# Issuing the probability-times-V products of up to three key blocks in one piece, in a two-layer transformer block whose instruction order a planner writes

## The chip, the cores and the metric

The kernel runs on one core of one Trainium2 chip. The metric is the device time of one execution in microseconds (us). Engines are named as the profile names them: PE is the matrix engine (TensorE), DVE is VectorE, ACT is ScalarE, POOL is GpSimd, SP is the engine whose queue issues every DMA here.

## What is computed

Two layers of a transformer block over 512 latent tokens (x) and 256 context tokens (ctx), 1024 wide, in float32. The context stream is left out after the attention keys of the second layer. Cut to what matters here:

```python
for layer in range(2):
    hx, hc = modulate(rmsnorm(x)), modulate(rmsnorm(ctx))
    # one projection, columns split into heads of 64 for three groups
    A: 6 query heads, 2 key heads; RMSNorm of q and k, rotary;  softmax(q k) v   over 768 keys
    B: 4 heads of two halves of 32; (softmax(q1 k1) - lam * softmax(q2 k2)) v, RMSNorm   over 768 keys
    C: 6 query heads, 2 key heads; 256 context keys and a band of three blocks of 128, plus a sink logit
    x += gate * (concat(A, B, C) @ w_out)                    # ctx likewise in layer 0
    x += gate * ((silu(h @ w1) * (h @ w3)) @ w2)             # ctx likewise in layer 0
return rmsnorm(x)
```

The modulation vectors come from `silu(c) @ w_ada`, 6144 columns a layer.

## The kernel before

The kernel doesn't call the engines as it goes. Every operation is recorded by a `Plan` as an `_Op` with its engine (or a choice of two: `act_dve` is ACT or DVE, `dve_pool` is DVE or POOL), its tiles and what it depends on. `schedule()` then walks through time with a price for each operation and picks, for the engine that is free first, the earliest operation that can start; operations of `together()` stay side by side. `issue()` emits the result, so all instructions have the line of its `getattr` in the profile (L347 before, L375 after the change), and rows are told apart by the names of the tiles. The order of the program is therefore decided by the prices, by the pools' sizes (`SLOTS`) and by a few offsets (`QK_AHEAD` lets score products run ahead of their place in the text).

Tiles: `u` is the pool of large SBUF buffers (4 KB a partition: weights, activations, probabilities P); `pt` holds transposed probabilities and, at the end of a layer's two halves, the gates (`gate`, read by DMA from `gscr`); `S` (2 buffers) and `T` (4 buffers of 512 columns) are in PSUM. Weights are loaded as `ws` and split into two parts `wh` and `wl` (a cast and a subtraction), and each product is made of three float32r products.

Attention goes by units: for A and B two query blocks of one pair of heads, for C one query block of all heads. Score products fill an S tile, DVE takes the maximum, ACT the exponent into P. Then P must be transposed: for each block of 128 keys PE transposes (matmuls against `ident`, 128 columns of output) into a T tile, ACT or DVE copies it to a `pt` tile, and PE multiplies V with it. One such product has 64 output partitions, so two of them (two heads) use the two halves of the array side by side; in the listing they are the rows `64x256` (A, B) and `64x384` (C), `128*64` in the profile. A product in float32 takes two passes, so a pair makes four rows in the profile. Here `acc` is the T tile that sums over key blocks:

```python
t = PT()
with plan.together():
    ...  # four transposes
pt = new("pt", [2, 256], "pt")
act_dve.copy(pt, t.rearrange("p (h n) -> p h n", h=2))
with plan.together():
    for h in range(2):
        pe.matmul(acc[64 * h:64 * h + 64, 0:256], lhsT=v_block(heads[h], kb), rhs=pt[:, h, :], ...)
```

The modulation uses products with 32 output partitions (`32x256`, four side by side). All other products have 128. In what follows a stretch of PE rows with the same number of output partitions, 64 say, between rows with another number is called a 64-row piece.

SP's queue is in order: a DMA that waits for a buffer holds up all DMAs behind it. After the last attention step of a layer come `gate_read` (the gates), the eight loads of `w_out` (`ws`), and the output projection (`T__1286`, `T__1287` are its first two result tiles in layer 0).

Of the kernel before, what the change touches and what calls it, by code (L numbers as in the profile page):

```python
# [16 lines left out]
PSUM = bass.MemoryType.PSUM  # L17
# [13 lines left out]
         "P1 P0 B P2 ABBBCAACAABCCCAAB"]  # L31
FF_TAIL = 3
FF_ADA = "dddd"
QK_AHEAD = 238
ADA_AHEAD = 300
SM_AHEAD = 39
# [4 lines left out]
COLS = {("a", "q"): (0, 384), ("a", "k"): (384, 128),  # L41
        ("b", "q0"): (640, 128), ("b", "q1"): (768, 128), ("b", "k"): (896, 256),
        ("c", "q"): (1408, 384), ("c", "k"): (1792, 128)}
SA = 0.125
SB = 32.0 ** -0.5
SLOTS = {"u": 41, "pt": 4, "s": 7, "y": 24, "rb": 2, "S": 2, "T": 4, "ropeG": 1}


class _Op:
    __slots__ = ("pos", "alts", "deps", "tiles", "dma", "gate", "tag", "boost",  # L50
                 "users", "left", "banks", "ready", "end", "eng", "calls", "at", "cost", "name")


class _Queue:
# [12 lines left out]
class Plan:  # L67
# [67 lines left out]
    def price(self, eng, method, args, kw):  # L135
        out = args[0]
        if method == "dma_start":
            return int(np.prod(out.shape)) * 4 / 360e3
        if method == "transpose":
            return 0.109  # L140
        if eng == "pe":
            n = kw["rhs"].shape[-1]
            if kw["rhs"].dtype == F32R:
                return n / 2400 + 0.003 if n >= 256 else 0.213
            share = {32: 4, 64: 2}.get(out.shape[0], 1)
            return max(n * 4 / 2400, 0.107) / share + 0.003
# [12 lines left out]
        return n * (2.5 if method == "tensor_tensor" else 1.0 if method == "memset" else 4.0) / 1200 + 0.1  # L159

    def any(self, alts):

        if self.group is not None:
            self.group.append(alts[0])
        else:
            self.add([(a[0], a, None) for a in alts])

    def add(self, alts):
        op = _Op()
        op.pos, op.tag = len(self.ops), self.label  # L170
        if alts[0][1] is None:
            calls = [o for _, _, o in alts]
            op.alts = [(calls[0][0], sum(self.price(*o) for o in calls), calls)]
        else:
            calls = [alts[0][1]]
            op.alts = [(e, self.price(*c), [c]) for e, c, _ in alts]
        op.dma = calls[0][1] == "dma_start"
# [47 lines left out]
    def schedule(self):  # L225
# [17 lines left out]
        free_at = dict.fromkeys(self.real, 0.0)  # L243
        cand = {e: [] for e in self.real}
        dma_free, now, frontier = 0.0, 0.0, 0
        done, order = [False] * n, []
# [14 lines left out]
        while len(order) < n:  # L261
            best = None
            for e in sorted(free_at, key=free_at.get):
# [4 lines left out]
                while heap and len(seen) < 250:  # L268
                    item = heapq.heappop(heap)
                    op = ops[item[1]]  # L270
                    if done[item[1]]:
                        continue
                    seen.append(item)
                    if op.gate > frontier:
                        continue
                    at, need = max(t0, op.ready, after_others(op, e)), {}
                    if any(e2 != e and max(free_at[e2], op.ready, now, after_others(op, e2)) + c2 < at + item[3]
                           for e2, c2, _ in op.alts):
                        continue
# [35 lines left out]
            if op.dma:  # L315
                free_at[e] = now + 0.5
                dma_free = max(now + 1.4, dma_free) + c
                op.end = dma_free + self.AFTER[e]
            else:
                free_at[e] = now + c  # L320
                op.end = now + c + self.AFTER[e]
            for b in op.banks:
                bank_end.setdefault(b, {})[e] = op.end
            order.append(op)
# [26 lines left out]
def dit_block(  # L351
# [26 lines left out]
    def new(tag, shape, name, dt=F32):  # L378
        return plan.tile(pools[tag], [128] + list(shape), dt, tag, nm(name))
# [10 lines left out]
    def PT():  # L390
        return new("T", [512], "T")
# [253 lines left out]
    for l in range(2):  # L645
# [33 lines left out]
        def v_block(h, kb):  # L679
            return V[kb // 2][:, kb % 2, 64 * h:64 * h + 64]  # L680
# [304 lines left out]

        def pv_pair(acc, Ps, off, heads, kbs):

            for n, kb in enumerate(kbs):
                t = PT()
                with plan.together():  # L990
                    for h in range(2):
                        for i in range(2):
                            pe.transpose(t[:, 256 * h + 128 * i:256 * h + 128 * i + 128],
                                         Ps[h][i][:, off + 128 * n:off + 128 * n + 128], ident)
                pt = new("pt", [2, 256], "pt")
                act_dve.copy(pt, t.rearrange("p (h n) -> p h n", h=2))
                with plan.together():
                    for h in range(2):
                        pe.matmul(acc[64 * h:64 * h + 64, 0:256], lhsT=v_block(heads[h], kb), rhs=pt[:, h, :],
                                  start=(n == 0), stop=(n == len(kbs) - 1))  # L1000

        def units(pairs):
            for p in pairs:
# [101 lines left out]
        def attn_c():  # L1105
# [4 lines left out]
            for r, i in ctx_first:  # L1110
# [46 lines left out]
                for n, kb in enumerate(kbs):  # L1157
                    pts = []
                    for g in range(2):
                        t = PT()  # L1160
                        with plan.together():
                            for j in range(3):
                                pe.transpose(t[:, 128 * j:128 * j + 128], Ps[g][j][:, 128 * n:128 * n + 128], ident)
                        pt = new("pt", [384], "pt")
                        act_dve.copy(pt, t[:, 0:384])
                        pts.append(pt)
                    with plan.together():
                        for g in range(2):
                            pe.matmul(acc[64 * g:64 * g + 64, 0:384], lhsT=v_block(6 + g, kb), rhs=pts[g],
                                      start=(n == 0), stop=(n == len(kbs) - 1))  # L1170
# [269 lines left out]
```

## Time and profile before

| | |
|---|---|
| median of 3 runs | 1753.08 us (1750.07 to 1755.17) |
| the profiled execution's own time | 1754.11 us |
| its span, first to last instruction | 1752.3 us |
| PE busy | 1697.7 us (97%) |
| DVE / ACT / POOL busy | 1208.2 (69%) / 615.2 (35%) / 218.1 (12%) us |
| mean granted clock of PE | 0.994 |

The rows below are from that one profiled execution. A row's busy time is from its start to its modelled end; matmuls overlap in the pipeline, so what one costs PE is read from start to start. "[0.62 <-ACT pt__1193]" behind a row is idle time of its engine before it and what ended it. Layer 0's attention lies at about 175 to 416 us, its feed-forward part at 416 to 1000, layer 1's attention at 1175 to 1345, its feed-forward part at 1390 to 1752.

### The profile page before, as it was taken

The page shows a single profiled execution, that of the slowest core. Times are in us where ns is not written, and L with a number is a line of the kernel's source. Part 1 is how long each engine was busy: PE and PEld are TensorE (multiplying, and loading weights), DVE is VectorE, ACT ScalarE, POOL GpSimd, SP SyncE. Part 2 cuts the span into 40 slices and gives each one's busy share as a digit, 9 for nine tenths or more (in the row PEclk, how much of TensorE's full clock was granted, in tenths as well). Part 3 has the DMA queues.
Part 4 walks back from the last instruction along what each step waited for, and adds up shares of the span by engine and source line. Part 5 has one row for each costly group of instructions (what it writes and reads, how often), then busy time and mean ns, then how long its engine had stood idle before and what let it go on. Part 6 is the DMA issues. An engine that isn't in the chain of part 4 may idle for free.

```text
span 1752.3 us, 24291 instructions
## 1 busy us (share of the span) xinstructions
PE 1697.7 (97%) x9426; PEld 1361.3 (78%) x9426; DVE 1208.2 (69%) x1950; ACT 615.2 (35%) x1280; POOL 218.1 (12%) x251
## 2 busy tenths in 40 slices
PE   6999898998999999999999999999999999999998
PEld 3787666676898888888888878877777888888886
DVE  3775878675567887576655765778876666676676
ACT  2523867663342122111101133157674411111111
POOL 0252200011000000000000521542001000000022
PEclk9999999999999999999999999999999999999999
DMA  9502220306363544254232342012005632332341
GB/s 314 188 27 84 67 85 20 96 11 171 96 200 101 169 159 148 93 191 136 69 108 89 105 145 72 13 31 68 1 1 157 180 109 75 106 109 81 112 144 48
DMA packets 153278, 182.96 MB, mean 104 GB/s; under 512 B 9316, under 2 KB 121396, under 8 KB 153164
## 3 DMA queue, kind: packets, MB, share of 16 engines
q1 hardware_dynamic: 153164, 181.42, 33.5%
q8 instruction: 74, 1.21, 0.3%
q14 instruction: 40, 0.33, 0.1%
HBM read 163.00 MB, written 9.47 MB: 98 GB/s over the span
## 4 chain that ended last, share of the span: by engine, by line
PE 86%; DVE 7%; issue 2%; POOL 2%; ACT 2%; DMA 2%; SPq 0%; DVEq 0%; POOLq 0%; ACTq 0%
DMA ws__1259<-in_w_out_dram 1%; PE S__1380 L347 0%; PE S__1379 L347 0%; PE S__1756 L347 0%; PE S__1561 L347 0%; PE S__1628 L347 0%; PE S__1881 L347 0%; PE S__1691 L347 0%; PE S__1823 L347 0%; PE S__1495 L347 0%; PE S__1995 L347 0%; PE S__1393 L347 0%; PE S__1967 L347 0%; PE S__1861 L347 0%; PE S__1853 L347 0%
## 5 line engine op out<-in xcount | busy, mean ns | idle before, releaser
L347 POOL TENSOR_TENSOR y__1397<-y__1397,gate__1998 128x512 f32<-128x512 f32 x1 | 1.3, 1297 | 481.0 <-DVE y__1397 L347 481.0
L347 POOL TENSOR_TENSOR ws__3491<-ws__3491,gate__3490 128x512 f32<-128x512 f32 x1 | 1.3, 1284 | 284.8 <-DMA ws__3491<-in_w_ff_dram 284.8
L347 DVE TENSOR_REDUCE t__2138<-sq__2137 128x6 f32<-128x384 f32 x1 | 0.6, 553 | 19.5 <-ACT sq__2137 L347 19.5
L347 ACT ACT_TABLE_LOAD x6 | 7.7, 1283 | 2.6 <-PE S__3040 L347 1.9
L347 ACT ACTIVATE sg__1860<-S__1853 128x768 f32<-128x768 f32 x1 | 0.8, 812 | 21.2 <-PE S__1853 L347 21.2
L347 ACT ACTIVATE sg__1914<-S__1907 128x768 f32<-128x768 f32 x1 | 0.8, 812 | 21.2 <-PE S__1907 L347 21.2
L347 ACT ACTIVATE sg__1940<-S__1933 128x768 f32<-128x768 f32 x1 | 0.8, 812 | 21.2 <-PE S__1933 L347 21.2
L347 ACT ACTIVATE sg__1966<-S__1959 128x768 f32<-128x768 f32 x1 | 0.8, 812 | 21.2 <-PE S__1959 L347 21.2
L347 DVE TENSOR_TENSOR sg__1994<-sg__1994,S__1995 128x768 f32<-128x768 f32 x1 | 1.0, 955 | 10.3 <-PE S__1995 L347 10.3
L347 ACT ACTIVATE sg__1793<-S__1786 128x768 f32<-128x768 f32 x1 | 0.8, 812 | 17.3 <-PE S__1786 L347 17.3
L347 ACT ACTIVATE sg__1665<-S__1658 128x768 f32<-128x768 f32 x1 | 0.8, 812 | 16.6 <-PE S__1658 L347 16.6
L347 PE MATMUL T__115<-wa__116,cstat 128*32 128x128 f32 x8 | 0.7, 418 | 5.7 <-DMA wa__116<-in_w_ada_dram 5.7
L347 ACT ACTIVATE xn__2033<-xf__2011 128x1024 f32<-128x1024 f32 x1 | 1.1, 1066 | 14.2 <-DVE xf__2011 L347 14.2
L347 POOL TENSOR_TENSOR ropeG<-ropeA,gqk 128x64 f32<-128x64 f32 (+1 forms) x12 | 6.0, 531 | 0.1
L347 ACT ACTIVATE sg__3107<-S__3102 128x512 f32<-128x512 f32 x1 | 0.6, 598 | 14.8 <-PE S__3102 L347 14.8
L347 ACT ACTIVATE sg__3459<-S__3454 128x512 f32<-128x512 f32 x1 | 0.6, 599 | 13.9 <-PE S__3454 L347 13.9
L347 ACT ACTIVATE sg__3173<-S__3168 128x512 f32<-128x512 f32 x1 | 0.6, 598 | 13.8 <-PE S__3168 L347 13.8
L347 ACT ACTIVATE sg__3195<-S__3190 128x512 f32<-128x512 f32 x1 | 0.6, 598 | 13.8 <-PE S__3190 L347 13.8
L347 ACT ACTIVATE sg__3217<-S__3212 128x512 f32<-128x512 f32 x1 | 0.6, 598 | 13.8 <-PE S__3212 L347 13.8
L347 ACT ACTIVATE sg__3239<-S__3234 128x512 f32<-128x512 f32 x1 | 0.6, 598 | 13.8 <-PE S__3234 L347 13.8
L347 ACT ACTIVATE sg__3261<-S__3256 128x512 f32<-128x512 f32 x1 | 0.6, 598 | 13.8 <-PE S__3256 L347 13.8
L347 ACT ACTIVATE sg__3283<-S__3278 128x512 f32<-128x512 f32 x1 | 0.6, 598 | 13.8 <-PE S__3278 L347 13.8
(14035 smaller groups left out, 6711.6 us busy)
## 6 DMA issues: line engine op xcount, KB each, us to landing
x__83<-in_x_dram SPq DMA_DIRECT2D x1, 512.0 KB
x__84<-in_x_dram SPq DMA_DIRECT2D x1, 512.0 KB
x__131<-in_x_dram SPq DMA_DIRECT2D x1, 512.0 KB, 5.9
x__136<-in_x_dram SPq DMA_DIRECT2D x1, 512.0 KB, 6.5
x__198<-in_ctx_dram SPq DMA_DIRECT2D x1, 512.0 KB
x__203<-in_ctx_dram SPq DMA_DIRECT2D x1, 512.0 KB
ws__241<-in_w_in_dram SPq DMA_DIRECT2D x1, 512.0 KB
ws__244<-in_w_in_dram SPq DMA_DIRECT2D x1, 512.0 KB
```

Source lines behind the costliest of these rows:

```text
L347: getattr(self.real[op.eng], method)(*args, **kw)
```

## The change

Three things change.

1. `pv_pair` and the loop in `attn_c` make transposes and copies for a run of key blocks first, and then record all V products of that run in one `together()`. `pv_runs` cuts the key blocks into equal runs of at most 3 (A, B) or 2 (C) blocks.
2. `pt` has 8 buffers in place of 4, `u` has 39 in place of 41.
3. The planner prices more: a change of the number of output partitions on PE costs `SWITCH` = 0.095 us in attention, and a PE candidate that stands more than `MODE_AHEAD` = 30 places further on isn't taken when the one found so far can start within `SWITCH`; an operation of DVE that reads two SBUF tensors (or copies within SBUF) and any operation of POOL are taken not to run at one time (`shares_port`); a float32r product of 512 columns is priced at 0.227 us in place of 0.216.

```diff
+PV_RUN = {"A": 3, "B": 3, "C": 2}
+SWITCH = 0.095
+MODE_AHEAD = 30
-SLOTS = {"u": 41, "pt": 4, "s": 7, "y": 24, "rb": 2, "S": 2, "T": 4, "ropeG": 1}
+SLOTS = {"u": 39, "pt": 8, "s": 7, "y": 24, "rb": 2, "S": 2, "T": 4, "ropeG": 1}
...
-                return n / 2400 + 0.003 if n >= 256 else 0.213
+                return (n + 32) / 2400 if n >= 256 else 0.213
...
+    def shares_port(self, eng, method, args, kw):
+        if eng == "pool":
+            return method != "dma_start"
+        if eng != "dve" or method == "memset":
+            return False
+        ins = [a for a in args[1:] if self.is_ap(a) and a.space != PSUM and int(np.prod(a.shape[1:])) > 1]
+        if method.startswith("tensor_scalar") or method == "tensor_copy":
+            return bool(ins) and args[0].space != PSUM
+        return len(ins) > 1
...
+                    if e == "pe" and soon is not None and item[0] > soon[1][0] + MODE_AHEAD and soon[0] <= t0 + SWITCH + 1e-9:
+                        break
...
+                    if e == "pe" and op.mode != mode and op.tag.startswith("att"):
+                        at += SWITCH
+                    if op.port[e]:
+                        at = max(at, port)
...
-            for n, kb in enumerate(kbs):
-                t = PT()
...
+            for n0, run in pv_runs(kbs, PV_RUN["A"]):
+                pts = []
+                for n in run:
+                    t = PT()
...
+                    pts.append(pt)
                 with plan.together():
+                    for n, pt in zip(run, pts):
+                        for h in range(2):
+                            pe.matmul(acc[64 * h:64 * h + 64, 0:256], lhsT=v_block(heads[h], kbs[n]), rhs=pt[:, h, :],
+                                      start=(n == 0), stop=(n == len(kbs) - 1))
+
+        def pv_runs(kbs, size):
+            m = -(-len(kbs) // size)
+            cuts = [len(kbs) * k // m for k in range(m + 1)]
+            return [(a, range(a, b)) for a, b in zip(cuts, cuts[1:])]
...
+                for n0, run in pv_runs(kbs, PV_RUN["C"]):
```

PE's order within a unit of group A in layer 0 (result tile `T__555`; `T__564` is a transpose of P, `S__618` and `S__667` are score tiles of units further on). Before:

```order
L347 MATMUL T__555<-pt__561,V__215 64x256 x2
L347 MATMUL T__564<-ident,P__543 128x128
L347 MATMUL T__564<-ident,P__549 128x128
L347 MATMUL T__564<-ident,P__544 128x128
L347 MATMUL T__564<-ident,P__550 128x128
L347 MATMUL S__618<-kx__456,qx__453 128x512
L347 MATMUL S__618<-kc__460,qx__453 128x256
L347 MATMUL S__618<-kx__457,qx__453 128x512
L347 MATMUL S__618<-kc__460,qx__453 128x256
L347 MATMUL T__555<-pt__563,V__215 64x256 x2
L347 MATMUL T__555<-pt__565,V__216 64x256 x2
```

Of the change, the same unit:

```order
L375 MATMUL T__555<-pt__557,V__214 64x256 x2
L375 MATMUL T__555<-pt__559,V__214 64x256 x2
L375 MATMUL T__555<-pt__561,V__215 64x256 x2
L375 MATMUL S__618<-kx__456,qx__453 128x512
L375 MATMUL S__618<-kc__460,qx__453 128x256
L375 MATMUL S__618<-kx__457,qx__453 128x512
L375 MATMUL S__618<-kc__460,qx__453 128x256
L375 MATMUL S__667<-kc__460,qc__458 128x256 x4
L375 MATMUL T__555<-pt__563,V__215 64x256 x2
L375 MATMUL T__555<-pt__565,V__216 64x256 x2
L375 MATMUL T__555<-pt__567,V__216 64x256 x2
```

The six pairs of `T__555` stood in five pieces and stand in two, of three pairs each; the transposes of a run now all stand ahead of its piece. Over the whole program PE has 121 64-row pieces before and 57 after, and 46 and 39 32-row pieces; the number of products is the same.

SP's order at the end of layer 0's attention (`gate` are reads of the gates, `ws` loads of `w_out`, `xr` loads of rows of the residual). Before:

```order
L347 DMA gate__1244<-gscr 128x512
L347 DMA ws__1247<-in_w_out_dram 64x1024 x2
L347 DMA ws__1250<-in_w_out_dram 64x1024 x2
L347 DMA xr__1283<-in_ctx_dram 128x1024
L347 DMA ws__1253<-in_w_out_dram 64x1024 x2
L347 DMA ws__1256<-in_w_out_dram 64x1024 x2
L347 DMA ws__1259<-in_w_out_dram 64x1024 x2
L347 DMA ws__1262<-in_w_out_dram 64x1024 x2
L347 DMA ws__1265<-in_w_out_dram 64x1024 x2
L347 DMA ws__1268<-in_w_out_dram 64x1024 x2
L347 DMA xr__1298<-in_ctx_dram 128x1024
L347 DMA gate__1245<-gscr 128x512
```

Of the change:

```order
L375 DMA gate__1243<-gscr 128x512
L375 DMA gate__1244<-gscr 128x512
L375 DMA gate__1245<-gscr 128x512
L375 DMA gate__1246<-gscr 128x512
L375 DMA ws__1247<-in_w_out_dram 64x1024 x2
L375 DMA ws__1250<-in_w_out_dram 64x1024 x2
L375 DMA xr__1283<-in_ctx_dram 128x1024
L375 DMA ws__1253<-in_w_out_dram 64x1024 x2
L375 DMA ws__1256<-in_w_out_dram 64x1024 x2
```

The third and fourth gate moved ahead of the loads of `w_out`. By the semaphores of the two programs, the second gate waited for the first V product of the last attention step (`T__1183`) before, and all four gates now wait for the first piece of the step ahead of it (`T__1137`).

## Rows read from the trace of the kernel before

**Rows 1.** The page: span, PE's busy time, and the chain that ended last.

```profile
span 1752.3 us, 24291 instructions
...
PE 1697.7 (97%) x9426; PEld 1361.3 (78%) x9426; DVE 1208.2 (69%) x1950; ACT 615.2 (35%) x1280; POOL 218.1 (12%) x251
...
PE 86%; DVE 7%; issue 2%; POOL 2%; ACT 2%; DMA 2%; SPq 0%; DVEq 0%; POOLq 0%; ACTq 0%
```

**Rows 2.** Windows: stretch, length, busy us of each engine (instructions), PE clock, DMA.

```profile
175.00:416.00 241.00, 222.12 (x1565) 153.96 (x1564) 179.48 (x373) 164.89 (x430) 29.34 (x39) 0.97 0.26 73
416.00:1000.00 584.00, 584.00 (x3202) 499.03 (x3201) 391.54 (x507) 123.53 (x171) 27.68 (x22) 1.00 0.40 127
...
1175.00:1345.00 170.00, 167.78 (x1145) 121.10 (x1144) 134.12 (x263) 122.18 (x292) 26.80 (x39) 1.00 0.20 49
...
1390.00:1700.00 310.00, 310.00 (x1391) 257.71 (x1391) 207.45 (x283) 53.51 (x69) 4.48 (x4) 1.00 0.38 116
```

**Rows 3.** Timeline of PE, layer 0's attention: start us, us, instruction, rows merged.

```profile
300.36 0.65 PE L347 MATMUL T__792<-pt__798,V__215 128*64 128x256 f32 x4
300.94 0.33 PE L347 MATMUL T__799<-ident,P__763 128*128 128x128 f32 x1
301.11 0.27 PE L347 MATMUL T__799<-ident,P__778 128*128 128x128 f32 x1
...
302.61 0.27 PE L347 MATMUL T__803<-ident,P__769 128*128 128x128 f32 x1
302.72 0.27 PE L347 MATMUL T__803<-ident,P__784 128*128 128x128 f32 x1
302.92 0.65 PE L347 MATMUL T__792<-pt__800,V__215 128*64 128x256 f32 x4
303.40 0.60 PE L347 MATMUL T__792<-pt__802,V__216 128*64 128x256 f32 x4
303.83 0.60 PE L347 MATMUL T__824<-pt__830,V__215 128*64 128x256 f32 x4
304.36 0.50 PE L347 MATMUL S__944<-kx__456,qx__455 128*128 128x512 f32 x1
304.70 0.28 PE L347 MATMUL S__944<-kc__460,qx__455 128*128 128x256 f32 x1
```

**Rows 4.** Chain that ended last: start us, us, what (24 products of 512 columns).

```profile
69.90 5.44 PE T__218 L347 x24
```

**Rows 5.** Waits of SP's queue, 300 to 425 us: total, times, longest.

```profile
SPq L347 <- PE T__1137 L347: 66.4, 1, 66.4
```

**Rows 6.** Timeline at the end of layer 0's attention.

```profile
392.57 1.16 SPq L347 DMA_DIRECT2D ws__1247<-in_w_out_dram  x2
...
406.67 0.50 PE L347 MATMUL T__1286<-wh__1248,oh__1284 128*128 128x512 f32 x1
...
409.09 1.04 ACT L347 CAST wh__1260<-ws__1259 128x1024 fp32r<-128x1024 f32 x1 [3.37 <-DMA ws__1259<-in_w_out_dram]
410.04 0.47 ACT L347 COPY pt__1240<-T__1239 128x384 f32<-128x384 f32 x1
...
410.57 0.80 PE L347 MATMUL T__1287<-wh__1248,oh__1284 128*128 128x512 f32 x1 [3.40 <-ACT pt__1240 L347]
```

**Rows 7.** Windows, columns as in rows 2.

```profile
410.00:415.00 5.00, 4.43 (x10) 2.29 (x11) 2.83 (x4) 2.66 (x5) 0.00 (x0) 0.50 1.02 245
```

**Rows 8.** Waits of PE, 175 to 416 us: total, times, longest.

```profile
PE S__822 L347 <- ACT P__784 L347: 1.2, 1, 1.2
...
PE T__746 L347 <- ACT pt__675 L347: 1.0, 1, 1.0
...
PE T__1198 L347 <- ACT pt__1193 L347: 0.6, 1, 0.6
```

**Rows 9.** Groups of instructions: xcount, busy us, mean ns, idle before.

```profile
L347 DVE TENSOR_TENSOR wl__2088<-ws__2086,wh__2087 128x1024 fp32r<-128x1024 f32 x1 | 2.3, 2308 | 0.0
```

**Rows 10.** Timeline of DVE, 405 to 407.5 us; POOL runs nothing there.

```profile
405.53 1.23 DVE L347 TENSOR_TENSOR wl__1255<-ws__1253,wh__1254 128x1024 fp32r<-128x1024 f32 x1
```

More of the change, by code (lines that the diff above doesn't have):

```diff
@@ L43 @@
         ("c", "q"): (1408, 384), ("c", "k"): (1792, 128)}
+SWITCH = 0.095
+MODE_AHEAD = 30
 SA = 0.125
 SB = 32.0 ** -0.5
-SLOTS = {"u": 41, "pt": 4, "s": 7, "y": 24, "rb": 2, "S": 2, "T": 4, "ropeG": 1}
+SLOTS = {"u": 39, "pt": 8, "s": 7, "y": 24, "rb": 2, "S": 2, "T": 4, "ropeG": 1}
 class _Op:
     __slots__ = ("pos", "alts", "deps", "tiles", "dma", "gate", "tag", "boost",
-                 "users", "left", "banks", "ready", "end", "eng", "calls", "at", "cost", "name")
+                 "users", "left", "banks", "ready", "end", "eng", "calls", "at", "cost", "name", "mode", "port")
 class _Queue:
@@ L176, in add @@
             op.alts = [(e, self.price(*c), [c]) for e, c, _ in alts]
+        op.mode = calls[0][2][0].shape[0] if calls[0][0] == "pe" else 0
+        op.port = {a[0]: self.shares_port(*(a[1] or calls[0])) for a in alts}
         op.dma = calls[0][1] == "dma_start"
@@ L245, in schedule @@
         dma_free, now, frontier = 0.0, 0.0, 0
+        mode, port = 128, 0.0
         done, order = [False] * n, []
@@ L321, in schedule @@
                 op.end = now + c + self.AFTER[e]
+            if e == "pe":
+                mode = op.mode
+            if op.port[e]:
+                port = now + c
             for b in op.banks:
@@ L986, in pv_pair @@
         def pv_pair(acc, Ps, off, heads, kbs):
-            for n, kb in enumerate(kbs):
-                t = PT()
-                with plan.together():
[L991 to L1000, printed above, removed]
+            kbs = list(kbs)
+            for n0, run in pv_runs(kbs, PV_RUN["A"]):
+                pts = []
+                for n in run:
+                    t = PT()
+                    with plan.together():
+                        for h in range(2):
+                            for i in range(2):
+                                pe.transpose(t[:, 256 * h + 128 * i:256 * h + 128 * i + 128],
+                                             Ps[h][i][:, off + 128 * n:off + 128 * n + 128], ident)
+                    pt = new("pt", [2, 256], "pt")
+                    act_dve.copy(pt, t.rearrange("p (h n) -> p h n", h=2))
+                    pts.append(pt)
+                with plan.together():
+                    for n, pt in zip(run, pts):
+                        for h in range(2):
+                            pe.matmul(acc[64 * h:64 * h + 64, 0:256], lhsT=v_block(heads[h], kbs[n]), rhs=pt[:, h, :],
[4 more added lines that the diff above has]
+            return [(a, range(a, b)) for a, b in zip(cuts, cuts[1:])]
         def units(pairs):
@@ L1156, in attn_c @@
                 kbs = [4, 5] + list(range(b0, b1))
[L1157 to L1166, printed above, removed]
+                for n0, run in pv_runs(kbs, PV_RUN["C"]):
+                    pts = {}
+                    for n in run:
+                        for g in range(2):
+                            t = PT()
+                            with plan.together():
+                                for j in range(3):
+                                    pe.transpose(t[:, 128 * j:128 * j + 128], Ps[g][j][:, 128 * n:128 * n + 128], ident)
+                            pts[n, g] = new("pt", [384], "pt")
+                            act_dve.copy(pts[n, g], t[:, 0:384])
                     with plan.together():
-                        for g in range(2):
-                            pe.matmul(acc[64 * g:64 * g + 64, 0:384], lhsT=v_block(6 + g, kb), rhs=pts[g],
-                                      start=(n == 0), stop=(n == len(kbs) - 1))
+                        for n in run:
+                            for g in range(2):
+                                pe.matmul(acc[64 * g:64 * g + 64, 0:384], lhsT=v_block(6 + g, kbs[n]), rhs=pts[n, g],
+                                          start=(n == 0), stop=(n == len(kbs) - 1))
                 for j, n in ((0, 1), (1, 2)) if r == 0 else ((0, 3),):
```

## Prediction

> **What bounds the kernel now.** I read the page first: PE is busy for 97% of the span and holds 86% of the chain that ended last [rows 1]. Then the windows by stage, since an average over the span mixes stages. In both feed-forward stretches PE is busy for the whole of the window (584.00 of 584 us, 310.00 of 310) [rows 2]: nothing there ends before PE's row work does, so only less PE work could shorten them, and the change takes none away there. In layer 0's attention PE is busy for 222.12 of 241 us, in layer 1's for 167.78 of 170, while DVE, ACT and POOL have room [rows 2]. So attention is bound by PE too, by the spacing of its rows and by some 19 us of gaps in layer 0. What the change can give is therefore the time by which PE rows stand further apart than the work in them asks (from start to start), and the gaps. The first I read from PE's timeline, the second from the waits and the end of layer 0.
>
> **Term A, the 64-row pieces.** In the timeline [rows 3] the piece from 302.92 holds three pairs. The middle pair takes 0.43 us from start to start (303.40 to 303.83), the first 0.48, the last, up to the next 128-row start, 0.53; the single pair at 300.36 takes 0.58. So a piece costs 0.05 + 0.10 = 0.15 us beyond its pairs. Next, its neighbours: a transpose ahead of the next transpose takes 0.11 us (302.61 to 302.72), the last one ahead of the piece 0.20 (302.72 to 302.92), which is 0.09 more. Behind the piece the first transpose takes 0.17 (300.94 to 301.11), 0.06 more; where a score product follows, its 512 columns take 0.34 (304.36 to 304.70) against 0.227 (5.44/24) in a dense run [rows 4], 0.11 more. A piece costs 0.30 us if transposes follow and 0.35 if anything else does. The order of the two programs says how many there are: 121 before, 53 with transposes behind and 68 with something else; 57 after, 6 and 51. That is 53 x 0.30 + 68 x 0.35 = 39.7 us before and 6 x 0.30 + 51 x 0.35 = 19.7 after: **-20**. The pairs themselves stay as many and keep 0.43. The bounds: the neighbours' share may belong to the transposes' place and not to the piece, then only 0.15 x 64 = 9.6 us go; or each piece may cost the larger 0.35, 22.4. I take 20, since the rows on both sides show the neighbours' share.
>
> **Term B, the 32-row pieces.** 46 become 39. No row of mine prices one; the nearest are the 64-row pieces at 0.30: 7 x 0.30 = **-2**, between 0 and -4 (twice the price).
>
> **Term C, the end of layer 0's attention.** SP's queue stood 66.4 us in one wait for `T__1137`, for a `pt` buffer of a gate [rows 5]; with a second wait for `T__1183` behind it, the first load of `w_out` was issued at 392.57 [rows 6]. The weights then come one after another: the fifth cast, on ACT, waited 3.37 us for its load until 409.09, the copy `pt__1240` stood behind it on ACT (410.04, 0.47 us), and PE, which needed that copy, was idle for 3.40 us before `T__1287` [rows 6]. In 410 to 415 us the granted clock was 0.50, that is 1.2 GHz, the lower level [rows 7]; PE's 4.43 busy us there would be some 2.2 at the upper one, so 2.2 more are lost. With waits such as the 0.6 us at `T__1198` [rows 8] the place costs 3.4 + 2.2 + some 1.8 = 7.4 us. Of the change, the third and fourth gate stand ahead of the loads, and none waits beyond `T__1137`'s first piece. From that piece to the first row of `T__1286` the order has 102 PE rows, 19 us at the prices of [rows 3, 4]; before, 14.1 us lay between the first load and that row (392.57 to 406.67 [rows 6]). The loads gain some 5 us, more than the 3.37 that the fifth was late. I take **-5**: the idle time and most of the slow stretch; bounds 0 (a later load is late instead, or two more gates ahead of them take up the lead) and -7.4.
>
> **Term D, new waits.** T has four tiles, one of them `acc`. A run of three transposes fills the other three, so work behind it waits for the copies (0.47 us each on ACT for a C block [rows 6]). By the order there are 31 places, 19 before, where less than 0.9 us of PE rows stand between a PE row and the later one that needs its copy or exponent. Waits of this kind took 0.6 to 1.2 us where they are largest [rows 8]. Twelve more at some 0.4 (near the copy's own 0.47) are **+5**; the bounds are 0 and 12 x 0.9 = +11. The piece itself seldom waits: only in 4 of 57 is there less than 1 us of PE rows between its last transposes and its first product.
>
> **What I cost at nothing.** The new port rule moves 84 elementwise operations from POOL to DVE (POOL 244 to 160, DVE 1064 to 1148). A subtraction of 128x1024 took 2.31 us on DVE at one place [rows 9] and 1.23 at another where POOL ran nothing [rows 10]; so DVE may win back what it takes on. DVE has 61 us free of 241 in layer 0's attention and 36 of 170 in layer 1's [rows 2], which hide it; if a chain to a copy or exponent runs through it, +-2. Two `u` buffers fewer may hold weight loads back in the feed-forward parts; there PE never waited [rows 2], and in both orders each load stands at least 18 us of PE rows ahead of its first use. The load, cast and subtraction take less: from the issue at 392.57 to the first product at 406.67 [rows 6], 14.1 us, was enough even with the queue just released. If that cover went, the late thing would be the cast of the next `ws`, in every step. The 8 `pt` buffers cost nothing but this.
>
> **Sum.** -20 - 2 - 5 + 5 = -22. The profiled execution took 1754.1 us, 1.0 above the median of the runs; 1754.1 - 22 = 1732.1, and from the median **1731**. The bounds of the terms are -22.4 to -9.6, -4 to 0, -7.4 to 0, 0 to +11 and +-2: together from 36 us less to 3 more. They are hardly all at one end; two of them part of the way give the likeliest case 1724 to 1740.
>
> **Rivals.**
> 1. *The copies eat half.* Term D at its bound (+11) and the end of layer 0 unmended (C at 0): -22 + 6 + 5 = -11, **1742**, 1740 to 1748 with the neighbours' share partly kept. For it: three transposes take some 4 x 0.11 x 3 = 1.3 us on PE and three copies, one behind another on one engine, 3 x 0.47 = 1.4, so copies just keep up if both ACT and DVE aren't busy. Against: score products stand in between nearly everywhere.
> 2. *No change.* The evacuation of PSUM sets the pace in attention, and what PE saves becomes idle time: 20 of the 22 us lost, about **1751**, 1748 to 1758. For it: ACT and DVE together copy all of T and read all of S. Against: DVE and ACT are busy 179 and 165 us where PE is 222, and in layer 1 134 and 122 of 168 [rows 2]; a saving of 12 us in layer 0 leaves PE well above both. The Trainium skill has a rule that speaks for this rival: by "TensorEngine Tiling (Array Packing)", section Performance Considerations, PSUM Bottleneck, tiling speeds up TensorE but not the copies out of PSUM, which may become the bottleneck, and both ScalarE and VectorE should be used for them. By that rule the sum would be about -2; the busy times of this trace don't agree with it, since neither engine reaches PE's load, and the copies are shared by both already.
> 3. *Slower.* The 39 `u` buffers hold back each step's weight loads in the feed-forward parts. There are 44 steps in the two stretches; the gain of 22 us is used up if PE waits 22/44 = 0.5 us in each, and at 0.65 us the time is about **1760**. For it: the buffers are 2 of 41, and SP's queue is in order. Against: no PE wait there before [rows 2], and the 18 us of lead.
> 4. *More.* The new waits don't come (D at 0) and the end of layer 0 is mended whole (C at -7.4): -20 - 2 - 7.4 = -29, and up to the bound of -35: **1718 to 1724**. For it: in the stretch of [rows 7] the clock was low behind an idle PE [rows 6], so what ends the idle time may end the low clock whole. Against: fewer buffers of T are free at any time, so some new wait is to be expected.
>
> **Chances.** Forecast (1724 to 1740) .62, rival 1 .20, rival 2 .07, rival 3 .04, rival 4 .07. The range leaves out rivals 2 and 3 and the far end of rivals 1 and 4: **1718 to 1747**. About what a measurement of this kernel can tell from no change is 0.3%, 5.3 us, 1747.8 to 1758.4: faster .89, same .07, slower .04.
>
> **What would show it.** PE's timeline should have pieces of two and three pairs at 0.43 us a pair, with 0.15 beyond, in half as many places; a piece longer than that, or transposes as far apart behind score products, would make A wrong. SP's long wait should end at `T__1137` and no wait follow it, the idle time before `T__1287` be gone and the granted clock there near 1. PE's waits for `pt` copies and for T tiles should sum to some 5 us more; at 11 or over it is rival 1. The feed-forward windows must stay full: a gap in each step would be rival 3. DVE's busy time may grow by little, POOL's must fall.

## The result, and the profile after the change

The changed kernel takes 1728.73 us (median of 4 runs, 1727.72 to 1733.27), beside 1754.12 us of the kernel before; the ratio is 0.9862, with a 95% interval of 0.9836 to 0.9889. The forecast was 1731 us.

The page of the changed kernel, in the parts of [rows 1]:

```profile
span 1726.1 us, 24221 instructions
...
PE 1677.6 (97%) x9426; PEld 1367.1 (79%) x9426; DVE 1189.7 (69%) x2036; ACT 617.2 (36%) x1278; POOL 128.9 (7%) x167
...
PE 87%; DVE 5%; ACT 3%; DMA 3%; issue 1%; SPq 1%; POOL 0%; DVEq 0%; POOLq 0%; ACTq 0%
```

PE is the bound as before, with the same 9426 matmuls and 20 us less busy time. POOL lost 89 us of work, but DVE, which took it on, is busy for 18.5 us less than before [rows 1].

The windows of the changed kernel, columns as in [rows 2]; the stages begin earlier now: layer 0's attention, its feed-forward part, layer 1's attention, its feed-forward part.

```profile
175.00:407.00 232.00, 216.94 (x1596) 160.43 (x1595) 178.25 (x385) 163.20 (x424) 26.73 (x35) 0.99 0.28 80
407.00:982.00 575.00, 575.00 (x3162) 491.43 (x3161) 388.01 (x513) 122.30 (x169) 7.15 (x9) 1.00 0.40 128
...
1107.00:1325.00 218.00, 207.98 (x1341) 161.10 (x1340) 167.93 (x363) 143.96 (x350) 33.91 (x50) 0.98 0.19 44
1370.00:1700.00 330.00, 330.00 (x1462) 273.42 (x1462) 222.74 (x307) 56.78 (x71) 7.64 (x5) 1.00 0.35 105
```

The feed-forward parts stay full, so two `u` buffers fewer cost nothing there. In the window of layer 1's attention PE is now not busy for 10.0 us; in the stretch of the kernel before that holds the same work it was 5.4:

```profile
1132.00:1350.00 218.00, 212.59 (x1338) 156.48 (x1338) 168.31 (x347) 143.95 (x348) 44.30 (x68) 0.98 0.18 44
```

**The span taken apart.** I took every PE row's distance to the next row's start and set beside it what that distance usually is (the 35th percentile over all 14 traces) for a row of its kind, with the same kind behind it and at the same place behind a change of the number of partitions. The usual distances add up to "spacing", what goes more than 15 ns beyond them to "gaps" (waits and stretches of low clock). Stages are cut at the first row of a tile that both kernels have (`T__389`, `T__1286`, `T__1324`, `S__1995`, `T__2119`, `T__2293`, `T__3002`). In us:

```
stage                               before: spacing gaps   after: spacing gaps   difference
up to layer 0's attention                    147.2  12.6           144.9  11.4   -2.3  -1.2
layer 0's attention                          214.6  28.5           204.6  29.3  -10.0  +0.8
its last step, output projection              42.4   6.0            41.5   0.2   -0.9  -5.8
feed-forward part                            554.2   2.6           555.6   1.3   +1.4  -1.3
between the layers                           127.1   9.5           126.4   4.7   -0.7  -4.8
layer 1's attention                          206.6   9.8           198.5  17.6   -8.1  +7.8
the rest                                     376.6   3.6           377.9   1.4   +1.3  -2.2
sum                                         1668.8  72.7          1649.3  66.0  -19.5  -6.7
```

The sum is 26.2 us, the difference of the spans (1752.3 - 1726.1); the 11 us ahead of PE's first row and behind its last, which no row takes in, stayed as they were. Some rows moved over the borders: six of 512 columns from layer 0's last step into its feed-forward part (in the -0.9 and the +1.4), six more out of layer 1's attention for six short ones (in the +1.3 and the -0.7), and four from ahead of layer 0's attention into it. So the spacing of a single stage is good to about 1 us, while the sum, with the same 9426 rows in both kernels, is untouched by it. The spacing of the two attention stages, -18.1, is what runs of V products were to give; the gaps come and go.

A run of three in the changed kernel's PE timeline (start us, us, instruction, rows merged):

```profile
291.95 0.27 PE L375 MATMUL T__801<-ident,P__784 128*128 128x128 f32 x1
292.46 0.65 PE L375 MATMUL T__792<-pt__794,V__214 128*64 128x256 f32 x4 [0.24 <-ACT pt__800 L375]
292.94 0.60 PE L375 MATMUL T__792<-pt__796,V__214 128*64 128x256 f32 x4
293.38 0.60 PE L375 MATMUL T__792<-pt__798,V__215 128*64 128x256 f32 x4
293.91 0.33 PE L375 MATMUL T__803<-ident,P__763 128*128 128x128 f32 x1
294.07 0.27 PE L375 MATMUL T__803<-ident,P__778 128*128 128x128 f32 x1
```

From start to start the pairs take 0.48, 0.44 and 0.53, and the first transpose behind them 0.16: the prices of [rows 3], paid once for three pairs. The wait of 0.24 us in brackets is one for a copy.

At the end of layer 0 the loads of `w_out` and the first row that uses them (SP, then PE), and the window behind it:

```profile
373.85 1.16 SPq L375 DMA_DIRECT2D ws__1247<-in_w_out_dram  x2
```

```profile
393.91 0.50 PE L375 MATMUL T__1286<-wh__1248,oh__1284 128*128 128x512 f32 x1
394.25 0.39 PE L375 MATMUL T__1287<-wh__1248,oh__1284 128*128 128x512 f32 x1
```

```profile
394.00:416.00 22.00, 22.00 (x102) 17.23 (x103) 12.97 (x21) 8.69 (x15) 0.56 (x1) 1.00 0.42 125
```

From the first load to `T__1286` there are now 20.1 us where there were 14.1 [rows 6]; `T__1287` follows in 0.34 us where PE had been idle for 3.40, and the granted clock is 1.00 where it had been 0.50 [rows 7].

### The profile page after: what moved, and what is told of

Read it like the earlier page. It is cut to its first block, busy times and chain, and to the rows that moved or that the text cites. A ratio compares the mean times of both kernels' runs of the same rounds, so it can differ in the third digit from the quotient of the medians.

```text
span 1726.1 us, 24221 instructions
## 1 busy us (share of the span) xinstructions
PE 1677.6 (97%) x9426; PEld 1367.1 (79%) x9426; DVE 1189.7 (69%) x2036; ACT 617.2 (36%) x1278; POOL 128.9 (7%) x167
## 4 chain that ended last, share of the span: by engine, by line
PE 87%; DVE 5%; ACT 3%; DMA 3%; issue 1%; SPq 1%; POOL 0%; DVEq 0%; POOLq 0%; ACTq 0%
DMA ws__2963<-in_w_out_dram 1%; SPq L375 1%; DMA ws__2951<-in_w_out_dram 1%; PE S__1380 L375 1%; PE S__1379 L375 1%; PE S__1756 L375 0%; PE S__1628 L375 0%; PE S__1561 L375 0%; PE S__1881 L375 0%; PE S__1691 L375 0%; PE S__1823 L375 0%; PE S__1495 L375 0%; PE S__1995 L375 0%; PE S__1993 L375 0%; PE S__1984 L375 0%
## 5 line engine op out<-in xcount | busy, mean ns | idle before, releaser
L375 ACT ACTIVATE xn__2033<-xf__2011 128x1024 f32<-128x1024 f32 x1 | 1.1, 1061 | 14.2 <-DVE xf__2011 L375 14.2
L375 ACT ACTIVATE sg__1994<-S__1993 128x768 f32<-128x768 f32 x1 | 0.8, 812 | 14.7 <-PE S__1993 L375 14.7
L375 ACT ACTIVATE sg__3195<-S__3190 128x512 f32<-128x512 f32 x1 | 0.6, 597 | 13.9 <-PE S__3190 L375 13.9
L375 ACT ACTIVATE sg__3305<-S__3300 128x512 f32<-128x512 f32 x1 | 0.6, 597 | 13.9 <-PE S__3300 L375 13.9
L375 ACT ACTIVATE sg__3415<-S__3410 128x512 f32<-128x512 f32 x1 | 0.6, 597 | 13.9 <-PE S__3410 L375 13.9
L375 ACT ACTIVATE sg__3129<-S__3124 128x512 f32<-128x512 f32 x1 | 0.6, 597 | 13.9 <-PE S__3124 L375 13.9
L375 ACT ACTIVATE sg__3239<-S__3234 128x512 f32<-128x512 f32 x1 | 0.6, 597 | 13.9 <-PE S__3234 L375 13.9
```

The lines of the kernel that those rows point to most:

```text
L375: getattr(self.real[op.eng], method)(*args, **kw)
```

## The experiments

The theory to test: a 64-row piece costs PE time wherever it stands (Theory 1). Its main rival: the planner's new prices rearranged the program and the runs matter little (Theory 2). Each ratio is to the kernel before, run beside it. "Spacing" and "gaps" are made for each trace as above.

```
kernel                                64-row   us      ratio [95%]              spacing gaps   gaps by attention: layer 0, 1
before                                 121                                      1668.8  72.7   28.5   9.8
after                                   57     1728.7  0.9862 [0.9836, 0.9889]  1649.3  66.0   29.3  17.6
e1_run1           runs of 1             83     1731.2  0.9869 [0.9856, 0.9883]  1657.6  59.4   23.4  15.1
e2_oldprices      old prices            65     1733.7  0.9882 [0.9869, 0.9896]  1653.7  67.7   22.2  16.7
e3_noport         no port rule          57     1744.3  0.9949 [0.9936, 0.9961]  1650.1  79.9   33.2  18.2
e4_slots          before, slots only   117     1752.0  0.9987 [0.9978, 0.9996]  1668.9  72.8   28.8  13.9
e5_split          pieces split          83     1740.0  0.9928 [0.9915, 0.9940]  1658.0  68.2   30.6  18.1
e6_run6           runs of 6 and 3       42     1717.9  0.9796 [0.9782, 0.9809]  1642.8  64.5   26.9  15.8
e7_noswitch       no SWITCH             64     1728.8  0.9862 [0.9849, 0.9875]  1652.2  62.2   25.9  18.8
e8_switchonly     before, SWITCH only   89     1759.6  1.0037 [1.0024, 1.0049]  1662.6  83.4   35.9  17.1
e9_pt4            old slots             66     1741.2  0.9937 [0.9924, 0.9949]  1653.4  75.7   37.9  17.6
e10_runs_only     before, runs only     66     1749.2  0.9978 [0.9969, 0.9987]  1654.6  83.0   40.5  12.3
e11_run6_noswitch                       43     1719.6  0.9812 [0.9798, 0.9825]  1644.0  62.6   27.1  17.8
e12_run6_pt10                           40     1727.5  0.9853 [0.9838, 0.9868]  1644.4  70.8   30.9  20.5
```

**e5_split, the price of a piece by itself.** The planner's result is left as it is, and only the first pair of a piece is issued ahead of the PE operation (a score product or a group of transposes) before it, where nothing depends on that:

```diff
+            ahead[x], op.calls = op.calls[:2], op.calls[2:]   # x: the PE operation ahead of the piece
...
             for k, op in enumerate(order):
+                for e, method, args, kw in ahead.get(k, ()):
+                    getattr(self.real["pe"], method)(*args, **kw)
```

> The changed kernel with the order of every engine as it is, but in 26 of its 57 pieces the first pair is issued one PE row earlier, ahead of the 128-row product or transposes that stood just before the piece: 83 pieces, no other row moved. Theory 1, a piece costs PE time by itself: +26 x 0.24 = +6 us by the closer rows that the changed kernel's trace shows, +8 by the 0.30 us of the prediction; 1735 to 1737 us. Rival, the number of pieces has no price and the gain lies in what the new order did elsewhere: 1729 us (1727 to 1731).

It took 1739.98 us, 11 us more than the changed kernel. 8.7 us of that is spacing: 0.33 us for each of the 26 pieces; the other 2.2 are gaps. One such place, in the changed kernel and then split (PE's timeline, L388 is the pair that moved):

```profile
295.10 0.39 PE L375 MATMUL S__946<-kx__456,qx__455 128*128 128x512 f32 x1
...
295.89 0.65 PE L375 MATMUL T__792<-pt__800,V__215 128*64 128x256 f32 x4
296.37 0.60 PE L375 MATMUL T__792<-pt__802,V__216 128*64 128x256 f32 x4
296.80 0.60 PE L375 MATMUL T__792<-pt__804,V__216 128*64 128x256 f32 x4
297.40 0.50 PE L375 MATMUL S__950<-kx__456,qx__455 128*128 128x512 f32 x1
```

```profile
298.71 0.65 PE L388 MATMUL T__792<-pt__800,V__215 128*64 128x256 f32 x4
299.29 0.50 PE L390 MATMUL S__946<-kx__456,qx__455 128*128 128x512 f32 x1
...
300.19 0.65 PE L390 MATMUL T__792<-pt__802,V__216 128*64 128x256 f32 x4
300.68 0.60 PE L390 MATMUL T__792<-pt__804,V__216 128*64 128x256 f32 x4
301.21 0.50 PE L390 MATMUL S__950<-kx__456,qx__455 128*128 128x512 f32 x1
```

The score rows and the three pairs take 2.30 us in one piece (295.10 to 297.40) and 2.50 in two (298.71 to 301.21), and the score rows themselves grow from 0.79 to 0.90. Theory 1 holds; that the number of pieces has no price falls.

**e1_run1 and e6_run6, other run lengths.**

```diff
-PV_RUN = {"A": 3, "B": 3, "C": 2}
+PV_RUN = {"A": 1, "B": 1, "C": 1}     # e1;  e6: {"A": 6, "B": 6, "C": 3}
```

> The changed kernel with runs of one key block (PV_RUN 1 for A, B and C); slots and prices as changed. PE has 83 64-row pieces by the order (57 in the changed kernel, 121 in the one before). Theory 1, each piece costs PE time: in the changed kernel's trace the attention rows stand closer by 15.6 us in all with 64 pieces less, 0.24 us each; 26 pieces more are +6 us, so 1735 us (1732 to 1738), and the waits of layer 1 (6.5 us more than before) may shrink again. Theory 2, the planner's prices give most of the gain and runs matter little: 1729 us (1727 to 1731).

> The changed kernel with runs of six key blocks (A, B) and three (C): 42 pieces. Theory 1 with waits unchanged: -15 x 0.24 = -3.6, 1725 us. Rival, a run of six goes twice through the three free T tiles, so transposes wait for the copies at 0.5 us each: the idle time of attention grows by more than the 3.6 us, 1729 us or more.

In e1 the spacing rose by 8.3 us for 26 pieces (0.32 each), so the price is there; but gaps fell by 6.6 us, 5.9 of them in layer 0's attention, and the time rose by only 2.5 us. Judged by its time, e1 cannot tell the theories apart; by its parts it fits Theory 1. It also shows that runs are not the only way to fewer pieces: with the buffers and the prices, but no runs, the planner leaves 83 of 121 pieces and e1 has 22.6 us of the gain, so on top of these the runs of the change add 2.5 at most, which the two intervals don't tell from nothing. In e6 spacing fell by 6.5 us for 15 pieces and two 32-row ones, gaps by 1.5; the median fell by 10.9 us to 1717.87 (the profiled spans, 1726.1 and 1718.5, by 7.6), better than my 1725 and with no sign of the copies that its rival expected. This version beats both kernels: its runs (1715.8 to 1720.3) lie below all of the changed kernel's.

**e4_slots, e9_pt4 and e10_runs_only: runs and buffers apart.** e4 has only the buffers, e10 only the runs, e9 all but the buffers:

```diff
-SLOTS = {"u": 39, "pt": 8, ...}
+SLOTS = {"u": 41, "pt": 4, ...}      # e8, e9 and e10; e4 is the kernel before with 39 and 8
```

> The kernel before with 8 buffers of pt and 39 of u only. 117 64-row pieces. Theory 1: the end of layer 0's attention is mended by the buffers alone, since all four gates then stand ahead of the loads of w_out and wait for an earlier step: -6 us there, and -1 for four pieces less: 1747 us (1745 to 1750), with PE's idle time ahead of T__1287 gone. Rival: the place needs the runs and prices too, or the feed-forward parts pay for two u buffers less: 1754 us or more.

> The changed kernel with the buffers of before (4 of pt, 41 of u): 66 64-row pieces. By the pieces alone +9 x 0.26 = +2 us, 1731 us. Theory A, 8 buffers of pt are needed so that a run's copies don't wait for the last run's products: PE's idle time in attention grows by several us, 1735 to 1742 us. Theory B, the idle times only follow the order and the buffers matter little: 1731 us, give or take the 5 us by which orders have differed.

> The kernel before with the runs only (4 of pt, 41 of u, old prices): 66 64-row pieces, 55 fewer than before, 48 32-row pieces. By the pieces -55 x 0.26 = -14 us: 1739 us. Where the loads of w_out are issued ahead of all gates, the end of layer 0's attention may be without its idle time too: 1733 us. If idle time in attention grows for want of pt buffers: 1745 us or more.

e4 mended the end of layer 0 in part (gaps there from 6.0 to 2.0 us) and got 4.1 us more of them in layer 1's attention: 1752.03, not the 1747 expected. e10 got its pieces (spacing -14.2) and lost 12.0 us to gaps in layer 0's attention. e9 shows the same from the other side, 8.6 us more of them than the changed kernel. So runs want the buffers: alone runs give 4 us and buffers 2, together (e2) 20. (The two pools were always changed together, so the shares of `pt` and `u` are not told apart by the times.) The place is around 260 us; one window of each, for the changed kernel, e9 and e6:

```profile
250.00:285.00 35.00, 29.76 (x188) 20.49 (x188) 28.05 (x43) 24.83 (x56) 0.40 (x1) 0.95 0.04 8
```

```profile
250.00:285.00 35.00, 26.98 (x129) 17.40 (x128) 27.91 (x45) 23.65 (x50) 0.88 (x2) 0.76 0.09 20
```

```profile
250.00:285.00 35.00, 29.50 (x191) 23.19 (x190) 29.50 (x53) 25.71 (x61) 3.43 (x4) 0.90 0.00 1
```

With 4 `pt` buffers PE issues 129 matmuls in these 35 us, at a mean clock of 0.76, where it issues 188 and 191 at 0.95 and 0.90 with 8. PE's timeline of e9 and of the changed kernel there:

```profile
258.62 0.80 PE L375 MATMUL S__693<-bkx__643,bqx__641 128*128 128x512 f32 x1 [0.70 <-ACT P__689 L375]
259.21 0.42 PE L375 MATMUL S__693<-bkc__645,bqx__641 128*128 128x256 f32 x1
259.99 0.80 PE L375 MATMUL S__700<-bkx__642,bqx__640 128*128 128x512 f32 x1 [0.37 <-ACT P__684 L375]
```

```profile
256.11 0.28 PE L375 MATMUL S__691<-bkc__645,bqx__640 128*128 128x256 f32 x1
256.32 0.65 PE L375 MATMUL T__745<-pt__747,V__214 128*64 128x256 f32 x4
...
258.53 0.60 PE L375 MATMUL T__745<-pt__757,V__216 128*64 128x256 f32 x4
259.06 0.50 PE L375 MATMUL S__693<-bkx__643,bqx__641 128*128 128x512 f32 x1
```

In e9 nothing stands between the score products from 257 to 271.8 us, and eight of these ten S tiles wait, each for an exponent that has to free one of the two buffers; the granted clock is 0.50 from 258.6 to 271.8 us, its lower level (1.2 GHz: 0.59 us from the first to the second score row, where it is 0.34 in [rows 3]). In the changed kernel six pairs, 2.7 us, stand between `S__691` and `S__693`. In e9 these six pairs of `T__745` start at 285.55. The second copy of their run tells why (e9, then the changed kernel):

```profile
282.78 0.69 DVE L375 COPY pt__749<-T__748 128x512 f32<-128x512 f32 x1
```

```profile
254.25 0.58 ACT L375 COPY pt__749<-T__748 128x512 f32<-128x512 f32 x1
```

The transposes of `T__748` end by 252 us in e9 too, yet its copy stands 31 us later, behind the six copies of another unit, `T__712`, at 272.9 to 280.9. It is the planner that holds it back: `schedule()` gives a tile no slot where the tiles that stand earlier in the text would then lack one, and with 4 buffers of `pt` the run of three of `T__712` and the first copy of `T__745` claim them all. With e9's buffers `schedule()` refuses `pt__749` for this reason even while three of the four stand empty. So here the four `pt` buffers hold up the copies through the planner's claims, and PE is left with score products; its own waits for copies into `pt` are only 0.6 us in layer 0's attention of e9, those for exponents that free an S tile 15.3 (10.2 in the changed kernel).

**e2, e3, e7, e8: the planner's prices.** e2 has the old prices with runs and buffers, e3 leaves out the port rule, e7 SWITCH and MODE_AHEAD; e8 adds only these two to the kernel before.

```diff
-        op.port = {a[0]: self.shares_port(*(a[1] or calls[0])) for a in alts}
+        op.port = {a[0]: False for a in alts}          # e2, e3, e8, e10
...
-SWITCH = 0.095
-MODE_AHEAD = 30
+SWITCH = 0.0
+MODE_AHEAD = 10 ** 9                                   # e2, e7, e10, e11
...
-                return (n + 32) / 2400 if n >= 256 else 0.213
+                return n / 2400 + 0.003 if n >= 256 else 0.213    # e2, e8, e10
```

> The changed kernel with runs and slots as changed but all prices of the planner as before (SWITCH 0, no MODE_AHEAD, no shared port, 0.216 us). 65 64-row pieces and 46 32-row pieces. Theory 1: the pieces cost +2 us, the 32-row ones +2, and the 8 us that were gained outside attention come back if they are due to the prices: 1733 us, up to 1741. Theory 2: most of the gain is lost, 1745 us or more.

> The changed kernel without the rule on the shared port only. 57 and 40 pieces. Theory A, the gain of some 8 us outside attention (start 2, between the layers 4, end 2, all idle time of PE) comes from keeping POOL from running beside DVE: it is lost, 1737 us (1734 to 1740). Theory B, it comes from other prices or from the new order: 1729 us (1727 to 1732).

> The changed kernel without SWITCH and MODE_AHEAD (runs, slots, port rule and the 0.227 us kept): 64 64-row pieces and 43 32-row pieces. By the pieces alone +7 x 0.24 and +4 x 0.3 = +3 us, 1732 us. If the order's idle times are what moves (as without the port rule, where PE's idle time rose by 14 us with the same pieces), it may be off this by 5 us or more either way, and the difference must stand in idle time, not in the spacing of the rows.

> The kernel before with SWITCH and MODE_AHEAD only (runs of one block, pt 4, u 41, no port rule): 89 64-row pieces, 32 fewer than before, 44 32-row pieces. Theory 1: -32 x 0.24 = -8 us, 1746 us, with the end of layer 0 as before. Theory 2, the planner's price is worth nothing without the buffers: 1752 us or more.

e2 (1733.67) keeps four fifths of the gain without any new price, so the prices are not what the gain rests on, and Theory 2 falls in that form. Its other half, that the runs matter little, is true only once prices and buffers are there (e1). Both ways to fewer pieces lose much of their worth to gaps where the buffers are missing (e8, e9, e10). e7 is the changed kernel's time: 7 more pieces and 4 more 32-row ones in spacing (+2.9), 3.8 less in gaps. e8 has 32 pieces fewer than the kernel before and is slower: spacing -6.2, gaps +10.7. I had expected 1746. e3 is off by more than either theory allowed: 13.9 us more of gaps than the changed kernel, of which 8.3 lie between the layers and 3.9 in layer 0's attention; why it is worse there than the old prices altogether (e2) I can't say.

What the port rule is worth can be seen between the layers. Of the kernel before, DVE and POOL at 1049 us and PE's wait (timeline):

```profile
1049.45 1.27 POOL L347 TENSOR_TENSOR xf__2015<-xf__2015,yg__2091 128x512 f32<-128x512 f32 x1
1049.52 1.75 DVE L347 TENSOR_SCALAR xn__2065<-xf__2014,t__2068 128x1024 f32<-128x1024 f32 x1
...
1051.33 0.33 PE L347 MATMUL T__2069<-ident,xn__2065 128*128 128x128 f32 x1 [1.40 <-DVE xn__2065 L347]
```

and the same operation in the changed kernel, in e3 its wait:

```profile
1026.98 0.75 DVE L375 TENSOR_SCALAR xn__2065<-xf__2014,t__2068 128x1024 f32<-128x1024 f32 x1
```

```profile
PE T__2069 L375 <- DVE xn__2065 L375: 2.5, 1, 2.5
```

Beside POOL the scaling took 1.75 us, alone 0.75. In e3 it took 0.75 as well, but late: the addition ahead of it stood on POOL (e3, first line), where the port rule has it on DVE (changed kernel, second line).

```profile
1032.72 2.15 POOL L375 TENSOR_TENSOR xf__2014<-xf__2014,yg__2064 128x512 f32<-128x512 f32 x1 [1.29 <-DVE yg__2064 L375]
```

```profile
1023.32 0.68 DVE L375 TENSOR_TENSOR xf__2014<-xf__2014,yg__2064 128x512 f32<-128x512 f32 x1
```

In all kernels with the port rule the gaps from `S__1995` to `T__2119` are 0.6 to 2.8 us, in all without it 4.1 to 7.4.

**e11 and e12, looking for more.**

> Runs of six (A, B) and three (C) without SWITCH and MODE_AHEAD: 43 64-row pieces against 42 with them, 38 32-row against 37. By the pieces 1718 us; without these prices the changed kernel had 3 us less idle time in layer 0's attention, so 1715 us (1712 to 1721).

> Runs of six and three with 10 buffers of pt and 38 of u: 40 64-row and 41 32-row pieces. If copies of the next run wait for pt buffers of the last one, idle time falls: 1713 us. If not, the pieces cancel (-2 and +4, some 0.3 us each): 1718 us.

e11 (1719.63) is e6 within their spread. e12 was a miss: spacing +1.6 and gaps +6.3 against e6, in both attention stages, so 10 `pt` buffers brought nothing over 8.

## Why the prediction was right

- **Terms A and B** (-20 and -2) measured -18.1 us of spacing in the two attention stages and -2.3 ahead of them, where five of the seven 32-row pieces went; over the whole program, where moved rows cancel, -19.5 of the -22. A piece is worth some 0.28 us from before to after (64 fewer) and 0.33 by e5, against 0.30 to 0.35 from the timeline.
- **Term C** (-5) measured -5.8 us of gaps, inside its bounds (the -0.9 of spacing there is rows that moved). SP's queue now waits 49.3 us for a copy (`pt__1143`) and 4.8 for `T__1137`, and the first load of `w_out` follows at 373.85; the 19 us that the order gave between load and use were 20.1. That the buffers mend it, by putting all gates ahead of the loads, was half true: e8 and e10, with 4 `pt` and two or all four gates behind the loads, also have 0.5 and 0.6 us of gaps there. What goes with the gaps is the distance from the first load to `T__1286`: it is 13.6 to 14.7 us in the three kernels with some 1.6 to 6 us of gaps (before, e4, e1), and 16.8 to 28.5 in the other eleven, which have 1.2 or less.
- **Term D** (+5) measured +8.6 (0.8 in layer 0, 7.8 in layer 1), but not by its mechanism. It expected 5 us more of waits for copies out of T behind runs of transposes. Sorted by what ended them, PE's waits for copies into `pt` fell in the two attention stages, from 3.8 us to 1.6, and those for other copies that free a T tile rose from 1.7 to 2.5. In layer 1's attention PE's idle time rose from 2.2 to 6.6 us, and the longest waits of the changed kernel (total, times, longest) are these:

```profile
PE T__2921 L375 <- DVE rb__2938 L375: 1.2, 1, 1.2
PE T__2479 L375 <- DVE bkx__2449 L375: 1.1, 1, 1.1
PE T__2480 L375 <- DVE bkc__2450 L375: 0.8, 1, 0.8
PE T__2376 L375 <- DVE rb__2393 L375: 0.8, 1, 0.8
```

Two are for factors (`rb`) that DVE prepares and PE reads. The other two are waits for a T tile after all, but for one that holds transposed queries and keys, not probabilities: `T__2479` doesn't read `bkx__2449`, it starts when the last cast out of `T__2454` has ended (1169.86).

```profile
1169.43 0.43 DVE L375 CAST bkx__2449<-T__2454 64x256 fp32r<-64x256 f32 x1 [0.43 <-ACT bkx__2448 L375]
```

```profile
1170.01 0.63 PE L375 MATMUL T__2479<-ident,stq__2477 128*128 128x128 f32 x4 [1.15 <-DVE bkx__2449 L375]
```

With 16 to 56 pieces there, layer 1's gaps were 9.8 us before and 12.3 to 20.5 in all other kernels, so the old order looks like a lucky one there; a count of the copies behind runs would not have found the step.
- **What I cost at nothing** was worth -4.8 us between the layers (by the rows above and e3, the port rule) and -2.2 at the end: that gap is 3.4 to 3.5 us in the five kernels with the price of 0.216 us and 1.3 in all with 0.227, e3 and e7 among them, which lack the other new prices in turn. I had seen the longer subtraction [rows 9, 10], and looked for its worth only in attention.
- **The sum.** By the spans the -22 should have been -26.2. These 7.0 us and the gaps of the start and of the feed-forward part (1.2 and 1.3) were left out, and term C was 0.8 short; against them A and B together had been 2.5 and D 3.6 too good. So 10.3 us of errors one way met 6.1 the other: that the forecast came within 3 us of the measured time is in part luck. The largest term is not: e5 bears out its price by itself.
- **The rivals.** Rival 1 did not come about: no wait for a copy into `pt` in attention is over 0.7 us, and layer 0's attention as a whole has 0.8 us more of gaps. Rival 2, that PE's saving turns into idle time, happened in layer 1 alone, where 7.8 of 8.1 us came back as gaps. The rule of the Trainium skill named there ("TensorEngine Tiling (Array Packing)", Performance Considerations, PSUM Bottleneck) says that copies out of PSUM may become the limit. The runs don't show such a limit: of the idle time in layer 1 only 2.2 us are waits for copies that free a T tile (0.6 before), and e10 and e6 went through the same stage with 5.3 and 5.7 us less in sum than the kernel before (spacing and gaps), the products and copies being as many. Rival 3 fell with the full feed-forward windows. Of rival 4 one half came, the end of layer 0 mended almost whole; the other, no new waits, did not.

## What to carry to other kernels

Price a change of the number of output partitions from the timeline at its borders, neighbours included. The pieces can be counted before a run: a straight line through the spacing of all 14 kernels gives 0.32 us a piece, and none lies more than 2.4 us off it (the worst is e8, whose 32 pieces fewer gave only 6.2 us). The gaps of an order written by a planner can't be added up like that: they moved by up to 14 us, over half the gain, with edits to a single setting, so an edit to such a planner is judged by spacing and gaps apart, and several neighbouring settings are worth running. An edit that groups work needs the buffers that let other work run in between; alone, either half was worth a tenth or two of both.

## Not expected of the hardware

A DVE scaling of 128x1024 took 1.75 us beside a POOL operation and 0.75 alone, and subtractions of 128x1024, which read two SBUF tiles, took 2.31 us (median of 9 that lay beside POOL for over nine tenths of their time) and 1.22 (median of 153 that lay beside none of its operations), both in the kernel before. DVE's additions and products of 128x512 took 0.69 us (median of 20 beside POOL) and 0.68 (of 452 beside none) there, but the median hides two kinds. The nine of the 20 that read a PSUM tile all took 0.68 to 0.69 beside POOL, and so did every such operation in the 14 traces (129, at most 0.69). Of the eleven that read SBUF alone, six took 0.68 to 0.69, one 0.95 and four 1.77 to 1.78. What tells these apart stands in their starts: the six had started 0.03 to 0.05 us ahead of POOL's operation, the five behind it, and the four longest ended 0.55 us after it had ended. In the 14 traces the 34 such operations that started ahead of POOL's took 0.70 us at most, the 37 that started behind it 0.67 (where POOL's ended 0.05 us later) to 1.78. So an operation of this kind waited out a POOL operation that had started before it, lost nothing to one that came later, and with one input in PSUM lost nothing at all.
